# The final norm's sums in token form between the last scatters, and a PSUM bank of their own for the router's sums

## The chip, the cores and the metric

The kernel runs on one core of one Trainium2 chip. Time is device microseconds (us) of one execution. Three timed runs of the kernel before gave 1637.0, 1640.71 and 1640.89 us; the median is 1640.71. A separate execution was profiled.

## The reference, cut to what matters

256 tokens of width 1024 pass through a first network (two layers of feed-forward, mixer, feed-forward) and a second block that ends in a mixture of experts and a final norm. Only the end of the second block is touched:

```
h2  = modulate(rmsnorm(x, g_ffn), sh2, sc2)
out = x + gt2 * hier_moe(h2)          # 32 experts in 4 groups, 2 experts per token
y   = modulate(rmsnorm(out, g_final), shf, scf)
rmsnorm(x, g) = x * rsqrt(mean(x*x, over the 1024 features) + 1e-6) * g
```

Both norms need, for each of the 256 tokens, the mean of 1024 squares, then the power -1/2 of it.

## The kernel before, in words

Activations lie with features on partitions: `self.x[0..7]` are eight tiles of 128 features x 256 tokens. A sum over features is therefore a sum over partitions, which TensorE does. There are two forms of it. In token form (`sums_tok`, line 432) a half of a square tile (128 features x 128 tokens) is the stationary operand and `mean1`, one column of 1/1024, the moving one; the result has tokens on partitions and one column for each half, so 2 columns. `rsqrt_tok` (438) adds epsilon on VectorE (tile `rtt`) and takes the power on GpSimd (tile `rte`), `bcast` (445) brings the two columns back to all partitions with two matmuls against the identity. In broadcast form, as `final` (2020) does it, `mean1` broadcast to 128 x 128 is stationary and the whole square tile moves; the result is the mean on every partition, 256 columns wide, and the power is taken on that form.

An fp32 matmul stands in the trace as two or more pieces. All matmul helpers go through one line, 233, so lines say little and tiles say more.

The router. `out_proj` calls `post2` (1608) for each of the 8 feature tiles. It adds to x, scales to `u`, squares into a running sum, and leaves a closure `later` that computes the router's logits (into the bank `pr`, tag p1, 36 columns a token half) and the transposes of `u`; a tile's closure is called in the next tile's `post2`, the last one by `block2` (1100). Before, the token sums of the norm went into columns 128 and 129 of the same bank `pr`, ahead of the last closure in the program. `moe` (1638) starts with `rsqrt_tok` on these two columns, scales the logits by it on VectorE, and picks groups and experts in a chain of small VectorE steps that ends in the mask `msk`. While VectorE does that, TensorE has `WARM[0]` matmuls without use (`keep_warm`, 1631). Then TensorE counts the mask into `pk` (tag p1 as well; each tag has two banks in turn), `WARM[1]` more follow, and the gather matmuls (`oh`, `hhi`, `hlo`) collect each expert's tokens.

The experts. `moe_round` (1899) runs 11 passes of 2 or 4 experts. Weights come in 1 MB loads on SP's queue, each into a buffer of a ring that a matmul frees. A pass has the up product, `mid`, the down product, which ends in `yh` (ScalarE) and `yl` (VectorE), and the scatter, which adds the result into four PSUM banks. The last pass is cut in quarters: `down` of quarter q is followed by the scatter of quarter q-1, two feature tiles each, and VectorE adds them to x. Before, `final` then squares x on ScalarE and sums it in broadcast form, behind the last `down` in TensorE's queue, takes the power, multiplies x by it, and applies gain and shift on ScalarE and GpSimd; five stores write the output. A loop after that runs another round when an expert has more tokens than its capacity.

Order on each engine is set by a scheduler that follows the program and the operands' readiness; `issue_after(ins)` puts what stands in it behind `ins` in that engine's queue.

Of the kernel before, what the change touches and what calls it, by code (L numbers as in the profile page):

```python
# [21 lines left out]
F32 = mybir.dt.float32  # L22
# [3 lines left out]
AF = mybir.ActivationFunctionType  # L26
OP = mybir.AluOpType
# [3 lines left out]
P = 128  # L31
S = 256
D = 1024
KD = 8
NFF = 22
EPS = 1e-6
# [5 lines left out]
BIG = 2.0 ** 20  # L42
OUT_POOL, OUT_ENDS = (1, 3, 5), (0, 2, 4, 6, 7)
X_LOADS = (0, 1), (2, 3, 4), (5, 6, 7), ()
WARM = 26, 5, 6
NEARLY = 2
NAHEAD = 10
NMORE = 3
# [133 lines left out]
class Net:  # L182
# [917 lines left out]
    def block2(self, post):  # L1100
        nc, A = self.nc, self.A
        rest = self.block2_in()
        with self.tc.tile_pool(name="b2", bufs=1, reuse_waits="tile") as bp:
            T = lambda n, shape, dt=F32: bp.tile(list(shape), dt, name="b2_" + n)
            y = [bp.tile([P, S], F32, tag="y", bufs=8, name=f"b2_y{c}") for c in range(8)]
            yb, yr = y[0:4], y[4:8]
            th = [self.xp.tile([P, S], F32, tag=f"x{c}", name=f"th{c}") for c in range(8)]
            th += [T(f"th{c}", (P, S)) for c in range(8, 16)]

            def sink(c, p):  # L1110
                self.act(th[c - 20], p[:, :S], AF.Tanh, scale=0.5)

            low = lambda: bp.tile([P, S], F32R, tag="y", bufs=8, name=self.name("b2_l"))

            def second(yl):

                for d in range(KD):
                    if d % 4 == 0:
                        w = self.split_w(A["pab"][2 + d // 4], 2048)
                    p = self.bank("p1")  # L1120
                    for k in range(4):
                        self.mm3(p[:, :S], *w((d % 4 * 4 + k) * P), *yl[k], k == 0, k == 3)
                    self.stt(th[2 * d + 1], th[2 * d + 1], 1.0, p[:, :S], op0=OP.add, op1=OP.mult)
                    if d % 2:
                        yield

            with self.tc.tile_pool(name="b2m", bufs=1, reuse_waits="tile") as mp:
                self.mixers2(mp, yr, yb, sink, rest, low, second)
            self.moe_pre()
            self.expert_ring(NAHEAD, "we")  # L1130
            with self.tc.tile_pool(name="b2o", bufs=1, reuse_waits="tile") as op:
                ya = [self.split_to((op.tile([P, S], F32R, name=f"b2_ha{c}"), low()), yr[c]) for c in range(4)]
                ms = [self.xhl(d) for d in range(KD)]
                for d in range(KD):
                    if d % 4 == 0:
                        w = self.split_w(A["pab"][d // 4], 2048)
                        self.expert_ahead(PABA)
                    p = self.bank(f"p{2 + d % 2}")
                    for k in range(4):
                        self.mm3(p[:, :S], *w((d % 4 * 4 + k) * P), *ya[k], k == 0, k == 3)  # L1140
                    t = self.tmp("t3")
                    self.stt(t, th[2 * d], 1.0, p[:, :S], op0=OP.add, op1=OP.mult)
                    tg = t, th[2 * d + 1]
                    m = self.tmp("sq", bufs=4)
                    self.tt(m, tg[0], tg[1], OP.add, eng=nc.gpsimd)
                    h, l = ms[d]
                    self.act(h, m, AF.Copy, scale=0.5)
                    self.stt(l, m, 0.5, h.bitcast(F32), op0=OP.mult, op1=OP.subtract)
                    if d == 5:
                        for k in range(KD):  # L1150
                            self.x[k] = self.xp.tile([P, S], F32, tag=f"x{k}", name=f"xr{k}")
                            nc.sync.dma_start(self.x[k], self.xd[:, k])
            self.out_proj(A["w_out2"], ms, lambda d, p: post(d, p, bp.tile([P, S], F32, tag="y", bufs=8, name=f"b2_u{d}")))
            self.summed = self.sums_tok(self.acc["n"], self.pr[:, 128:130], False)
            self.later()
            self.spare = self.bank("p2"), ms[0][0]

    def mixers2(self, mp, yr, yb, gate, rest, low, second):
# [472 lines left out]
    def keep_warm(self, n):  # L1631
# [4 lines left out]
        return last  # L1636

    def moe(self, final):
        nc, A = self.nc, self.A
        pr = self.pr  # L1640
        rt = self.rsqrt_tok(pr[:, 128:130], EPS, 2)
        self.rings += [(self.st, "s")] * 3 + [(self.xp, "xl")]
        self.expert_ahead()
        self.wkb_es.close()
# [2 lines left out]
        with self.tc.tile_pool(name="moe", bufs=1, reuse_waits="tile") as mp:  # L1647
# [4 lines left out]
            n = [0]  # L1652
# [56 lines left out]
            with self.tc.issue_after(self.summed.ins):  # L1709
                self.keep_warm(WARM[0])  # L1710
            pk = self.bank("p1")
# [6 lines left out]
            with self.tc.issue_after(counted.ins):  # L1718
                self.keep_warm(WARM[1])
            self.rc = T("rc", (P, 4, 32))  # L1720
# [58 lines left out]
                return order  # L1779

            self.moe_round(weights)
            self.spare = self.bank("p1"), self.yh
            with self.tc.issue_after(self.scattered.ins):
                self.keep_warm(WARM[2])
            final()
            n_more = nc.values_load(nxi[0:1, 0:1], min_val=0, max_val=3)
            with self.tc.For_i(0, n_more, 1):
# [111 lines left out]
    def moe_round(self, early=None):  # L1899
# [69 lines left out]
        def down(n, c0=0, c1=D, w=None):  # L1969

            (heT, _, cs), (p, m, cap) = mids[n], PASSES[n]
            w = w or self.expert_get(*[(1, p + i, 0) for i in range(m)])
            for c in range(c0, c1, 512):
                e = min(c + 512, c1)
                py = self.bank("p0")
                for f in range(2):
                    for i in range(m):
                        last = self.mm(py[i * cap:(i + 1) * cap, 0:e - c], heT[:, f * P + i * cap:f * P + (i + 1) * cap],
                                       w[i].rearrange("p (q f c) -> p f q c", f=2, c=256)[:, f, c // 256:e // 256], f == 0, f == 1)
                self.act(self.yh[:, c:e], py[:, 0:e - c], AF.Copy, scale=cs)  # L1980
                self.stt(self.yl[:, c:e], py[:, 0:e - c], cs, self.yh.bitcast(F32)[:, c:e], op0=OP.mult, op1=OP.subtract)
            return w, last

        def scatter(n, ds=range(KD)):
            ohT = mids[n][1]
            for d in ds:
                o = acc[d // 2][:, (d % 2) * S:(d % 2 + 1) * S]
                first, last = n == 0 and d % 2 == 0, n == N - 1
                self.mm(o, self.yh[:, d * P:(d + 1) * P], ohT, first, False)
                self.scattered = self.mm(o, self.yl[:, d * P:(d + 1) * P], ohT, False, last)  # L1990
# [16 lines left out]
            if n < N - 1:  # L2007
                down(n)
        w = None
        for q in range(5):  # L2010
            if q < 4:
                w, last = down(N - 1, q * 256, (q + 1) * 256, w)
            if q:
                with self.tc.issue_after(last.ins):
                    scatter(N - 1, (2 * q - 2, 2 * q - 1))
                for d in (2 * q - 2, 2 * q - 1):
                    self.stt(self.x[d], acc[q - 1][:, (d % 2) * S:(d % 2 + 1) * S], self.M(5)[:, d:d + 1], self.x[d])
        self.downed = last

    def final(self, out):  # L2020
        p = self.bank("p1")
        sq = []
        for k in range(KD):
            sq.append(self.xp.tile([P, S], F32, tag=f"xh{k}", name=self.name("sq")))
            self.act(sq[-1], self.x[k], AF.Square)
        with self.tc.issue_after(self.downed.ins):
            for k in range(KD):
                self.mm(p[:, :S], self.mean1.to_broadcast([P, P]), sq[k], k == 0, k == KD - 1)
        ms, r = self.tmp("t0"), self.tmp("t1")
        self.ts(ms, p[:, :S], EPS, op0=OP.add)  # L2030
        self.tt(r, ms, self.mhalf.to_broadcast([P, S]), OP.pow, eng=self.nc.gpsimd)
        o = self.st.tile([P, KD, S], F32, tag="s", name=self.name("o"))
        for k in range(KD):
            ok = o[:, k]
            self.tt(ok, self.x[k], r, OP.mult)
            g, b = self.gF[:, k:k + 1], self.M(6)[:, k:k + 1]
            if k in OUT_POOL:
                self.ts(ok, ok, g, b, op0=OP.mult, op1=OP.add, eng=self.nc.gpsimd)
            else:
                self.act(ok, ok, AF.Identity, bias=b, scale=g)  # L2040
            if k in OUT_ENDS:
                a = max([-1] + [e for e in OUT_ENDS if e < k]) + 1
                self.nc.sync.dma_start(out[:, a:k + 1], o[:, a:k + 1])
# [180 lines left out]
```

## Time and profile before

| | before |
|---|---|
| median of the timed runs | 1640.71 us |
| the profiled execution, and its span | 1642.62 us, 1640.9 us |
| TensorE busy | 1530.8 us, 93% |
| VectorE busy | 1049.1 us, 64% |
| ScalarE busy | 696.9 us, 42% |
| GpSimd busy | 362.3 us, 22% |
| mean granted TensorE clock | 0.973 |
| DMA | 344.33 MB, mean 210 GB/s |

Times are in microseconds from the start of the span. PE is TensorE, PEld its weight load, DVE VectorE, ACT ScalarE, POOL GpSimd, SP the engine that issues most DMAs (SPq its queue). A busy TensorE isn't TensorE at its peak, since matmuls are pipelined. The granted clock (PEclk) is 1.00 at the upper of two levels and 0.50 at the lower one.

### The profile page before, as it was taken

What the parts mean: (1) busy time and instruction counts of PE and PEld (TensorE: products, weight loads), DVE (VectorE), ACT (ScalarE), POOL (GpSimd) and SP (SyncE); (2) the same over time, 40 slices, a digit from 0 to 9 for tenths busy, and PEclk for the clock granted to TensorE, in tenths of its full rate; (3) what the DMA queues carried; (4) which work ended last, traced back from release to release, by engine and by line L of the source; (5) the groups of instructions that cost most, each with busy time, mean ns of one, the idle gap of its engine ahead of it and who ended that gap; (6) DMA issues with size and microseconds to landing.
All of it is one profiled execution on the core that took longest, in us unless ns stands there. A gap on an engine that the chain in (4) does not pass through costs nothing.

```text
span 1640.9 us, 29888 instructions
## 1 busy us (share of the span) xinstructions
PE 1530.8 (93%) x11892; PEld 1359.1 (83%) x11892; DVE 1049.1 (64%) x1938; ACT 696.9 (42%) x1241; POOL 362.3 (22%) x338
## 2 busy tenths in 40 slices
PE   8999998999999999999999999998999989999760
PEld 8999996799999999999879999988888886444330
DVE  6777776867876577766987777657875474322120
ACT  5444444544444444444554456444474332111010
POOL 4131222132221112111122221233221130000027
PEclk9999999999999999999999999999999999999985
DMA  8675554145755567545334774463421298999940
GB/s 302 247 270 202 200 197 155 52 136 212 277 216 175 200 232 275 204 169 182 120 109 165 268 274 170 142 246 107 156 65 52 78 373 319 376 420 420 420 185 27
DMA packets 62482, 344.33 MB, mean 210 GB/s; under 512 B 11136, under 2 KB 15360, under 8 KB 28544
## 3 DMA queue, kind: packets, MB, share of 16 engines
q1 hardware_dynamic: 59520, 340.65, 56.2%
q8 instruction: 95, 1.56, 0.4%
q0 software_dynamic: 640, 1.57, 0.4%
q10 hardware_dynamic: 2176, 0.13, 0.1%
q14 instruction: 51, 0.42, 0.1%
HBM read 339.05 MB, written 2.36 MB: 208 GB/s over the span
## 4 chain that ended last, share of the span: by engine, by line
PE 69%; issue 15%; DVE 8%; POOL 4%; ACT 2%; DMA 1%; SPq 0%; ACTq 0%; DVEq 0%; POOLq 0%
PE ps L233 68%; POOL t L239 3%; DVE l L239 2%; PE ps L236 1%; ACT h L258 1%; DVE xl L248 1%; DVE t L239 0%; POOL rte L239 0%; DVE xh L243 0%; DMA s<-in_ev_win 0%; DVE t L248 0%; POOL sq L239 0%; POOL kne L239 0%; DVE x L239 0%; DMA x<-in_xT 0%
## 5 line engine op out<-in xcount | busy, mean ns | idle before, releaser
L233 PE MATMUL ps<-xh,h 128*128 128x256 f32 x1992 | 570.2, 286 | 12.1 <-ACT h L258 7.3
L233 PE MATMUL ps<-xh,l 128*128 128x256 f32 x1992 | 570.0, 286 | 0.2 <-DVE l L239 0.2
L233 PE MATMUL ps<-xl,h 128*128 128x256 f32 x1992 | 569.0, 286 | 0.4
L258 ACT ACTIVATE h<-s 128x1024 fp32r<-128x1024 f32 (+4 forms) x419 | 401.5, 960 | 366.0 <-PE ps L233 291.1
L239 DVE TENSOR_TENSOR l<-s,h 128x1024 fp32r<-128x1024 f32 (+4 forms) x416 | 464.7, 1125 | 139.5 <-ACT h L258 137.8
L233 PEld LDWEIGHTS ps<-xh,h 128*128 128x128 f32 x1992 | 380.5, 191 | 17.1 <-ACT h L258 6.8
L233 PEld LDWEIGHTS ps<-xh,l 128*128 128x128 f32 x1992 | 380.4, 191 | 6.1 <-DVE l L239 2.1
L233 PEld LDWEIGHTS ps<-xl,h 128*128 128x128 f32 x1992 | 380.8, 191 | 1.7 <-DVE xl L248 1.2
L239 POOL TENSOR_TENSOR t<-t,t 128x256 f32<-128x256 f32 x93 | 121.2, 1304 | 399.0 <-DVE t L239 338.3
L233 PE MATMUL ps<-ah,h 128*128 128x256 f32 x704 | 201.4, 286 | 0.0
L233 PE MATMUL ps<-ah,l 128*128 128x256 f32 x704 | 199.3, 283 | 0.1
L233 PE MATMUL ps<-al,h 128*128 128x256 f32 x704 | 199.1, 283 | 0.0
L233 PEld LDWEIGHTS ps<-ah,l 128*128 128x128 f32 x704 | 134.9, 192 | 0.4 <-DVE l L239 0.3
L233 PEld LDWEIGHTS ps<-al,h 128*128 128x128 f32 x704 | 135.0, 192 | 0.0
L233 PEld LDWEIGHTS ps<-ah,h 128*128 128x128 f32 x704 | 134.9, 192 | 0.0
L233 PE MATMUL ps<-we,gT 128*32 128x512 f32 (+1 forms) x512 | 98.8, 597 | 7.6 <-DMA we<-in_w 7.6
L239 DVE TENSOR_TENSOR t<-ps,rb 128x256 f32<-128x256 f32 x196 | 81.8, 420 | 32.3 <-PE ps L233 24.7
L239 POOL TENSOR_TENSOR t<-t,mhalf 128x256 f32<-128x256 f32 x1 | 41.1, 41127 | 223.2 <-DVE t L243 223.2
L258 ACT ACTIVATE ah<-t 128x256 fp32r<-128x256 f32 x88 | 36.7, 417 | 117.2 <-POOL t L239 117.2
L239 DVE TENSOR_TENSOR al<-t,ah 128x256 fp32r<-128x256 f32 x88 | 37.9, 431 | 64.0 <-ACT ah L258 64.0
L239 POOL TENSOR_TENSOR sa<-sa,sq 128x256 f32<-128x256 f32 x34 | 41.9, 1232 | 149.8 <-ACT sq L258 149.4
L233 PEld LDWEIGHTS ps<-we,gT 128*32 128x32 f32 (+1 forms) x512 | 25.9, 119 | 58.4 <-issue 43.1
(490 smaller groups left out, 2162.2 us busy)
## 6 DMA issues: line engine op xcount, KB each, us to landing
s<-in_ffn_gu SPq DMA_DIRECT2D x87, 1024.0 KB
we<-in_w SPq DMA_DIRECT2D x64, 1024.0 KB
s<-in_ffn_dn SPq DMA_DIRECT2D x64, 704.0 KB
we<-in_w2e SPq DMA_DIRECT2D x28, 1024.0 KB
s<-in_w_ada SPq DMA_DIRECT2D x24, 1024.0 KB
s<-in_w_in SPq DMA_DIRECT2D x18, 1024.0 KB
s<-in_w_ada_f SPq DMA_DIRECT2D x8, 1024.0 KB
s<-in_ev_win SPq DMA_DIRECT2D x7, 1024.0 KB
```

What stands on the lines that cost most here:

```text
L233: return self.nc.tensor.matmul(out, lhsT, rhs, start=start, stop=stop, skip_group_check=True)
L236: self.nc.tensor.transpose(out, in_, ident)
L239: return (eng or self.nc.vector).tensor_tensor(out, a, b, op=op)
L248: self.nc.vector.scalar_tensor_tensor(out, a, s, b, op0=op0, op1=op1)
L258: self.nc.scalar.activation(out, a, f, **kw)
```

## The change

`final`'s norm goes to token form: `moe_round` squares x and sums it in three groups of feature tiles (0 to 3 behind the scatter of tiles 4 and 5, then 4 and 5 behind the last scatter, then 6 and 7), `final` takes the power of 2 columns and broadcasts it. The router's sums get a bank of tag p1, and the last `later` closure is queued behind them. The counts of warming matmuls change, and the last ones move from `moe` into `moe_round`, behind the sums.

```
-WARM = 26, 5, 6
+WARM = 40, 6, 4
 # block2
-            self.summed = self.sums_tok(self.acc["n"], self.pr[:, 128:130], False)
-            self.later()
+            self.sums = self.bank("p1")
+            self.summed = self.sums_tok(self.acc["n"], self.sums)
+            with self.tc.issue_after(self.summed.ins):
+                self.later()
 # moe
-        rt = self.rsqrt_tok(pr[:, 128:130], EPS, 2)
+        rt = self.rsqrt_tok(self.sums[:, 0:2], EPS, 2)
...
             self.moe_round(weights)
-            self.spare = self.bank("p1"), self.yh
-            with self.tc.issue_after(self.scattered.ins):
-                self.keep_warm(WARM[2])
             final()
 # moe_round
-        for q in range(5):
+        p = self.bank("p1")
+        for q in range(6):
             if q < 4:
                 w, last = down(N - 1, q * 256, (q + 1) * 256, w)
-            if q:
+            if 0 < q < 5:
                 with self.tc.issue_after(last.ins):
                     scatter(N - 1, (2 * q - 2, 2 * q - 1))
                 for d in (2 * q - 2, 2 * q - 1):
                     self.stt(self.x[d], acc[q - 1][:, (d % 2) * S:(d % 2 + 1) * S], self.M(5)[:, d:d + 1], self.x[d])
-        self.downed = last
+            for d in {3: (0, 1, 2, 3), 4: (4, 5), 5: (6, 7)}.get(q, ()):
+                sq = self.xp.tile([P, S], F32, tag=f"xh{d}", name=self.name("sq"))
+                self.act(sq, self.x[d], AF.Square)
+                with self.tc.issue_after(self.scattered.ins):
+                    for j in range(2):
+                        summed = self.mm(p[:, j:j + 1], sq[:, j * P:(j + 1) * P], self.mean1, d + j == 0, d == KD - 1)
+        self.sums = p
+        self.spare = self.bank("p1"), self.yh
+        with self.tc.issue_after(summed.ins):
+            self.keep_warm(WARM[2])
 # final
-        p = self.bank("p1")
-        for k in range(KD):
-            sq.append(self.xp.tile([P, S], F32, tag=f"xh{k}", name=self.name("sq")))
-            self.act(sq[-1], self.x[k], AF.Square)
-        with self.tc.issue_after(self.downed.ins):
-            for k in range(KD):
-                self.mm(p[:, :S], self.mean1.to_broadcast([P, P]), sq[k], k == 0, k == KD - 1)
-        self.ts(ms, p[:, :S], EPS, op0=OP.add)
-        self.tt(r, ms, self.mhalf.to_broadcast([P, S]), OP.pow, eng=self.nc.gpsimd)
+        pb = self.bcast(self.rsqrt_tok(self.sums[:, :2], EPS, 2), "p0")
...
-            self.tt(ok, self.x[k], r, OP.mult)
+            self.tt(ok, self.x[k], pb[:, :S], OP.mult)
```

## Rows read from the trace of the kernel before

**Rows 1.** Windows: busy us (count) per engine, granted clock, DMA share, GB/s.

```profile
1400.00:1408.00 8.00, 8.00 (x38) 2.62 (x35) 1.59 (x3) 1.47 (x3) 0.00 (x0) 1.00 0.55 209
1408.00:1572.00 164.00, 152.20 (x932) 68.89 (x930) 37.94 (x97) 22.23 (x42) 0.00 (x0) 1.00 1.01 419
1587.70:1628.80 41.10, 0.00 (x0) 0.00 (x0) 0.00 (x1) 0.00 (x0) 41.06 (x1) 0.54 0.00 1
```

**Rows 2.** Waits of SP's queue, 1362 to 1412: total us, times, longest.

```profile
SPq L1874 <- PE ps L233: 27.8, 7, 11.9
```

**Rows 3.** Timeline of GpSimd and VectorE: start, us, instruction, [idle before <- releaser].

```profile
1307.46 1.01 POOL L239 TENSOR_TENSOR gne<-gnt,mhalf 128x4 f32<-128x4 f32 x1 [32.12 <-DVE gnt L243]
...
1587.64 41.13 POOL L239 TENSOR_TENSOR t<-t,mhalf 128x256 f32<-128x256 f32 x1 [223.22 <-DVE t L243]
1628.80 2.97 DVE L239 TENSOR_TENSOR o<-xr,t 128x256 f32<-128x256 f32 x8 [41.24 <-POOL t L239]
```

**Rows 4.** Timeline of the last scatters, squares and sums, three engines.

```profile
1580.94 0.28 PE L233 MATMUL ps<-t,yl 128*128 128x256 f32 x1
1581.79 0.38 PE L233 MATMUL ps<-t,yh 128*128 128x256 f32 x1 [0.57 <-ACT yh L258]
...
1582.53 0.28 PE L233 MATMUL ps<-t,yh 128*128 128x256 f32 x1
1582.65 0.28 PE L233 MATMUL ps<-t,yl 128*128 128x256 f32 x1
...
1583.48 3.61 PE L233 MATMUL ps<-sq,mean 128*128 128x256 f32 x16
...
1582.17 1.68 DVE L248 SCALAR_TENSOR_TENSOR xr<-ps,mod,xr 128x256 f32<-128x256 f32 x4
1587.13 0.43 DVE L243 TENSOR_SCALAR t<-ps 128x256 f32<-128x256 f32 x1 [3.29 <-PE ps L233]
...
1582.68 1.61 ACT L258 ACTIVATE sq<-xr 128x256 f32<-128x256 f32 x4 [0.94 <-DVE xr L248]
```

**Rows 5.** Timeline of the router's sums, warming matmuls and epsilon.

```profile
1362.45 0.50 PE L233 MATMUL ps<-mean,sq 128*128 128x1 f32 x4
...
1363.26 0.31 PE L236 MATMUL ps<-con,b_u 128*128 128x128 f32 x1
1363.32 3.35 PE L233 MATMUL ps<-xh 128*128 128x256 f32 x26
...
1363.47 0.16 DVE L243 TENSOR_SCALAR rtt<-ps 128x2 f32<-128x2 f32 x1 [1.51 <-PE ps L233]
```

**Rows 6.** Timeline of two powers and their broadcasts at block 2's start.

```profile
1074.70 0.69 POOL L239 TENSOR_TENSOR rte<-rtt,mhalf 128x2 f32<-128x2 f32 x1
...
1074.77 1.61 PE L233 MATMUL ps<-con,rte 128*128 128x128 f32 x8 [1.24 <-POOL rte L239]
...
1075.52 0.38 ACT L258 ACTIVATE rb<-ps 128x256 f32<-128x256 f32 x1 [3.14 <-PE ps L233]
```

**Rows 7.** Instructions by tile: ns shortest/median/longest, first and last start.

```profile
L239 POOL TENSOR_TENSOR rte<-rtt,mhalf x9: 685/722/1797, 18.1 to 1363.7; 128x2 f32<-128x2 f32 x9
...
L239 DVE TENSOR_TENSOR t<-ps,rb x196: 403/419/426, 22.3 to 1003.7; 128x256 f32<-128x256 f32 x196
...
L239 DVE TENSOR_TENSOR o<-xr,t x8: 410/418/617, 1628.8 to 1631.4; 128x256 f32<-128x256 f32 x8
```

**Rows 8.** Windows of the first gather, and after the last sums.

```profile
1369.40:1372.70 3.30, 3.21 (x14) 3.02 (x14) 3.24 (x13) 0.83 (x2) 0.00 (x0) 0.50 0.99 410
1587.10:1591.50 4.40, 0.00 (x0) 0.00 (x0) 0.43 (x1) 0.00 (x0) 3.86 (x1) 0.96 0.03 7
```

**Rows 9.** Timeline of TensorE: the mask's count and the first gather.

```profile
1368.41 0.19 PE L233 MATMUL ps<-moe_msk,masks 128*128 128x64 bf16 x1 [1.74 <-DVE moe_msk L239]
...
1370.39 0.58 PE L233 MATMUL ps<-oh,hlo 128*128 128x256 f32 x1
...
1372.95 0.28 PE L233 MATMUL ps<-oh,hlo 128*128 128x256 f32 x1
```

More of the change, by code (lines that the diff above doesn't have):

```diff
@@ L2017, in moe_round @@
                     self.stt(self.x[d], acc[q - 1][:, (d % 2) * S:(d % 2 + 1) * S], self.M(5)[:, d:d + 1], self.x[d])
-        self.downed = last
-    def final(self, out):
-        p = self.bank("p1")
-        sq = []
-        for k in range(KD):
-            sq.append(self.xp.tile([P, S], F32, tag=f"xh{k}", name=self.name("sq")))
-            self.act(sq[-1], self.x[k], AF.Square)
-        with self.tc.issue_after(self.downed.ins):
-            for k in range(KD):
-                self.mm(p[:, :S], self.mean1.to_broadcast([P, P]), sq[k], k == 0, k == KD - 1)
-        ms, r = self.tmp("t0"), self.tmp("t1")
-        self.ts(ms, p[:, :S], EPS, op0=OP.add)
-        self.tt(r, ms, self.mhalf.to_broadcast([P, S]), OP.pow, eng=self.nc.gpsimd)
+            for d in {3: (0, 1, 2, 3), 4: (4, 5), 5: (6, 7)}.get(q, ()):
[8 more added lines that the diff above has]
+            self.keep_warm(WARM[2])
+    def final(self, out):
+        pb = self.bcast(self.rsqrt_tok(self.sums[:, :2], EPS, 2), "p0")
         o = self.st.tile([P, KD, S], F32, tag="s", name=self.name("o"))
```

## The prediction

> **What bounds the kernel now.** I read the windows of the expert stage first [rows 1]. From 1408 to 1572 us the DMA engines are full (share 1.01, 419 GB/s): the experts' weights set the pace. Just before, from 1400 to 1408, they are at 0.55, and the load queue's waits of 1362 to 1412 [rows 2] name TensorE (27.8 us in 7 waits): a load goes out when a matmul has freed its buffer. So what the router's part of TensorE gains before 1408 is handed on to the load stream and from there to the end. The third window, 1587.7 to 1628.8, holds one instruction: TensorE 0, ScalarE 0, GpSimd 41.06 of 41.10 us. The timeline names it [rows 3]: a power of 41.13 us on GpSimd, and 0.03 us after its end VectorE's first output multiply, which had waited 41.24 us for it. From there to the end of the span, 1640.9, are 12.1 us of output stage and stores. Two stretches decide the change: the router, 1361 to 1373, and the end, from 1580.
>
> **The power.** The old one has all 256 tokens in the columns of every partition; the new one has tokens on partitions and 2 columns. Three widths stand in the trace [rows 3, 7]: 2 columns 0.72 us (the median of nine, 0.69 to 1.80), 4 columns 1.01, 256 columns 41.13. From 2 to 4 a column costs 0.15 us, from 2 to 256 it costs (41.13 - 0.72) / 254 = 0.159: the time is in the columns. The one of 4 columns came after 32.12 us of idle GpSimd, so idleness isn't it. Nothing lies beside these 41 us. Removed: 40.4 us; 39.3 if the new one is as slow as the slowest of the nine.
>
> GPSIMD Engine Reference, section "Elementwise — side-by-side cycle accounting", in the Trainium skill gives a two-input elementwise instruction about 2.6 cycles an element at 1.2 GHz. By it 256 columns would be 0.55 us (an estimate from that page), 40 us would be no matter of columns, and the edit would save half a microsecond; for this operation [rows 3, 7] contradict it, and what it would mean is rival C. Perfetto Trace Analysis, section "GPSIMD Engine Instruction", also in the Trainium skill, calls a GpSimd instruction's span unreliable; here VectorE's start right at its end [rows 3] confirms the 41 us by another engine.
>
> **The sums ahead of it.** Before, TensorE ends the last scatter at 1582.65 + 0.28 = 1582.93, does 6 warming matmuls, then 16 pieces of sums, 1583.48 to 1587.09; VectorE adds epsilon from 1587.13, and the power starts at 1587.64 [rows 4, 3]. After, a square has four pieces of one column; such a group took 0.50 us at the router [rows 5], so eight squares need 4.0 us, no less than the 3.61 of before. What is won is place: the sums of the first four squares (2.0 us) can go behind the second-last scatter, which ends at 1580.94 + 0.28 = 1581.22. TensorE then waited 0.57 us for its operand [rows 4]; that gap hides a part, the rest delays the last scatter. In numbers: these sums to 1583.22; the last scatter's four matmuls 0.12 apart, the first two done at 1583.62, all at 1583.86; VectorE's two last additions (1.68 / 4 = 0.42 each) end at 1584.5, ScalarE's two last squares (1.61 / 4 = 0.40) at 1584.95. TensorE is later than that: sums of squares 4 and 5 to 1584.86, of 6 to 1585.36, of 7 to 1585.86. Then two columns of epsilon (0.16, [rows 5]) and the power, each with 0.05 to 0.07 to start: the power runs from 1586.14 to 1586.85, 1.5 us earlier than now.
>
> Added behind the power: the broadcast back over partitions, two fp32 matmuls. At 1074 us the same step was 0.75 us from TensorE's start to ScalarE's read of its result [rows 6]; with 0.05 to start, 0.80, and the first multiply is at 1587.65 instead of 1628.80: minus 41.15. The multiplies now read PSUM; that costs nothing (0.419 us from PSUM, 0.418 from SBUF, [rows 7]), so the last 12.1 us stay. Queued behind the multiplies are the same ScalarE and GpSimd steps and the five stores as before; no DMA is added or moved.
>
> Bounds of this part. Best: the last scatter isn't delayed, squares end at 1582.68 + 1.61 = 1584.29 and only the last group stands behind them: the power 1.1 us earlier than worked out, minus 42.2. Worst: all eight groups after the last square (4.0 us from 1584.95, 3.1 later than worked out), the slowest power (1.1 more) and the broadcast at half clock (0.75 more): minus 36.2. Half clock is possible since TensorE has little to do around the power; but before, after its last matmul at 1587.1, the granted clock was still 0.96 over the next 4.4 us [rows 8], and the gap will now be about 1 us.
>
> The four warming matmuls (4 x 0.13 = 0.5 us, from 3.35 / 26 in [rows 5]) stand between the sums and the broadcast while epsilon and power run (0.99 us): hidden, 0.5 us if not. The bank for the sums, p1, and the one for the broadcast, p0, belong to expert outputs read before: no wait.
>
> **The router.** Before, the sums share a bank with the router's logits, and the epsilon step starts at 1363.47, though the last sums end at 1362.45 + 0.50 = 1362.95 [rows 5]: it waits for the last logits in the same bank. With a bank of their own, and `later` queued behind them, it can start at 1363.0: 0.47 us earlier, and with it the chain to the mask, which let TensorE's count go at 1368.41 [rows 9]. The logits and transposes moved behind the sums keep their end, about 1363.5, and are needed at 1363.9; if they came later than that, they would eat the gain. `pk` now reuses the logits' buffer instead of a fresh one; its last reader is done microseconds before.
>
> The warming matmuls go from 26 to 40. The 26 ran from 1363.32 to 1366.67; then TensorE did nothing for 1.74 us [rows 9], and from 1369.4 to 1372.7 its granted clock was 0.50, the lower of its two levels, 1.2 GHz [rows 8]. The 40 last 40 x 0.129 = 5.15 us, to 1368.5, and issue until about 1368.2. The mask is ready at 1367.9: it waits 0.3 us behind them, so TensorE gains 0.2 us there. If the clock then stays at 2.4 GHz, the gather's 13 matmuls from 1370.39 to 1372.95, 0.213 us apart [rows 9], go 0.12 apart as in the last scatter: 12 x 0.093 = 1.1 us. I take 1.2 for both together, handed on whole to the load stream [rows 1, 2]. Bounds: 0.47 + 1.1 = 1.6 gained, or 0.1 lost, if the clock falls all the same and 14 x 0.129 = 1.8 us of new matmuls fill a gap of 1.74.
>
> **Sum.** 41.15 + 1.2 = 42.4 us off the profiled execution, 1642.6 (span 1640.9): 1600.2. That execution lay 1.9 us above the median 1640.7, so 1598.3 on the median's scale; I say 1598. With both parts at their ends it would be 1596.9 to 1604.6; the shown runs go down to 1637.0, 3.7 us below the median.
>
> **Rivals.**
> A. The sums stay late: TensorE's queue has them all behind the last scatter, or the squares come late on ScalarE. For: the squares stand on ScalarE's queue among the last `yh` steps, and a queue in order can stand before an operand. Against: the edit ties the first group to the second-last scatter alone. Price 3.1 us and up to 0.75 for the clock: 1602.
> B. The router gains nothing, that is, the change does not keep the clock there: the 1.74 us gap is filled, but one-column sums and other small matmuls surround it. Price 1.2: 1599.5.
> C. The 41 us are not in the columns. The power would still take 41.13, start 1.5 us earlier, have 0.8 us behind it, and the router give 1.2: 1640.7 - 1.9 = 1638.8, no change to be seen. Against: [rows 3, 7].
> D. Slower: a second expert round. The loop after the output runs once for each capacity overflow, now never. If the router's sums, moved from a bank that the logits open to one that they open themselves, came out otherwise, a count over its capacity (64, for the smaller experts 32) would start a round: from the first gather matmuls, about 1369.5, to the last addition, 1583.85, 214 us, and a second output stage of some 14: 1598 + 228 = 1826. It decides from one token over capacity. Against: the same products are added in the same order.
>
> **How the numbers follow.** Forecast 0.62, A 0.14, B 0.20, C 0.02, D 0.02. The range goes from 1637.0 - 42.4 = 1594.6 to A and a little over it, 1602.5, and holds B. About 0.3% (4.9 us) is what a measurement of this kernel can tell from no change: faster 0.96 (forecast, A, B), same 0.02 (C), slower 0.02 (D).
>
> **What would show it.** In the profile after: a two-column GpSimd power of about 0.7 us near 1585; eight groups of one-column sums, four of them ahead of the last scatter; VectorE's first multiply about 0.8 us after the power; the output stage still 12 us. At the router: the epsilon step some 0.5 us earlier, no TensorE gap before the count, a granted clock of 1.00 through the first gather, and the full DMA stretch starting about 1.2 us earlier. The prediction is wrong if the last power keeps more than a few microseconds, if the sums all stand behind the last scatter (A), or if the load stream does not move with the router (B).

## The result, and the profile after

Four timed runs of the changed kernel gave 1599.18 to 1602.66 us, median 1601.87, beside 1639.22 (1637.0 to 1640.89) for the kernel before: ratio 0.977, 95% interval 0.9751 to 0.9789. In a second series it was 1598.53 beside 1639.67, ratio 0.9749 (0.9727 to 0.9771). The profiled execution took 1602.33 us, its span is 1600.6. The gain is 37 us in the one series and 41 in the other.

Busy time by engine on the page after (share of the span, count of instructions):

```profile
PE 1533.1 (96%) x11925; PEld 1361.7 (85%) x11925; DVE 1049.0 (66%) x1938; ACT 696.7 (44%) x1241; POOL 320.6 (20%) x338
```

Only GpSimd changed by much: 362.3 - 320.6 = 41.7 us less. The power is 40.43 of them; most of the rest is its three steps of the output stage, which take 1.80 us together instead of 2.83. VectorE's multiplies beside them now read PSUM; no run shows whether that is why. GpSimd's timeline before, then after:

```profile
1629.74 2.83 POOL L245 TENSOR_SCALAR o<-o,pre_gF,mod 128x256 f32<-128x256 f32 x3 [0.98 <-DVE o L239]
1588.09 1.80 POOL L245 TENSOR_SCALAR o<-o,pre_gF,mod 128x256 f32<-128x256 f32 x3 [2.25 <-DVE o L239]
```

The router after the change, timeline of VectorE and TensorE, against [rows 5, 9]; the first line is the router's last addition to x, from which I count:

```profile
1361.92 0.48 DVE L248 SCALAR_TENSOR_TENSOR xr<-ps,mod,xr 128x256 f32<-128x256 f32 x1 [2.59 <-PE ps L233]
...
1363.77 0.16 DVE L243 TENSOR_SCALAR rtt<-ps 128x2 f32<-128x2 f32 x1 [0.98 <-PE ps L233]
...
1364.22 5.03 PE L233 MATMUL ps<-xh 128*128 128x256 f32 x40
1369.09 0.20 PE L233 MATMUL ps<-moe_msk,masks 128*128 128x64 bf16 x1
...
1372.42 0.28 PE L233 MATMUL ps<-oh,hlo 128*128 128x256 f32 x1
```

The epsilon step (`rtt`) starts 1.85 us after the addition; the count has no idle time in brackets any more. The last `oh,hlo` of the gather comes 3.33 us after the count's start (before 1372.95 - 1368.41 = 4.54).

Windows after: the gather, the stretch before the full DMA engines, the full stretch, and two about the last power (columns as in [rows 1]):

```profile
1369.40:1372.70 3.30, 3.08 (x24) 2.72 (x25) 3.28 (x13) 0.84 (x2) 0.00 (x0) 1.00 1.01 417
1400.00:1408.00 8.00, 8.00 (x39) 2.94 (x36) 1.94 (x5) 1.76 (x3) 0.00 (x0) 1.00 0.63 233
1408.00:1572.00 164.00, 152.68 (x932) 68.79 (x931) 37.75 (x96) 22.17 (x42) 0.00 (x0) 0.99 1.01 419
1584.90:1585.90 1.00, 0.70 (x5) 0.40 (x4) 0.15 (x1) 0.00 (x0) 0.70 (x1) 0.61 0.00 0
1585.90:1587.10 1.20, 1.20 (x4) 0.91 (x4) 0.00 (x0) 0.00 (x0) 0.00 (x0) 0.50 0.00 0
```

The clock over the gather is 1.00 instead of 0.50 [rows 8]; the expert stage still runs at the DMA engines' full share. The last two windows, 0.61 and 0.50, were not foreseen. The load stream follows the router, as predicted: SP's issue of the two loads just ahead of the full stretch starts 43.33 us behind the router's last addition before and 41.95 after, 1.38 earlier (SP's timeline before, then after):

```profile
1404.41 2.93 SPq L1874 DMA_DIRECT2D we<-in_w2e  x2
1403.87 2.93 SPq L1873 DMA_DIRECT2D we<-in_w2e  x2
```

The end after, timelines of TensorE, VectorE and GpSimd, against [rows 3, 4]:

```profile
1580.24 0.28 PE L233 MATMUL ps<-t,yl 128*128 128x256 f32 x1
1580.36 1.84 PE L233 MATMUL ps<-mean,sq 128*128 128x1 f32 x16
1582.06 0.36 PE L233 MATMUL ps<-t,yh 128*128 128x256 f32 x1
...
1582.62 0.95 PE L233 MATMUL ps<-mean,sq 128*128 128x1 f32 x8
1583.80 1.05 PE L233 MATMUL ps<-mean,sq 128*128 128x1 f32 x8 [0.24 <-ACT sq L258]
1584.72 0.86 PE L233 MATMUL ps<-yh 128*128 128x256 f32 x4
1585.89 1.22 PE L233 MATMUL ps<-con,rte 128*128 128x128 f32 x4 [0.30 <-POOL rte L239]
...
1584.89 0.16 DVE L243 TENSOR_SCALAR rtt<-ps 128x2 f32<-128x2 f32 x1 [1.20 <-PE ps L233]
1587.15 2.74 DVE L239 TENSOR_TENSOR o<-xr,ps 128x256 f32<-128x256 f32 x8 [2.09 <-PE ps L233]
...
1585.13 0.70 POOL L239 TENSOR_TENSOR rte<-rtt,mhalf 128x2 f32<-128x2 f32 x1 [220.41 <-DVE rtt L243]
```

The first line is the last matmul of the second-last scatter; four groups of sums (16 pieces) stand right behind it, then the last scatter, then the other four. The power takes 0.70 us instead of 41.13.

The same points, read from the timelines of every run, cut the span into stages whose sum is the span. X is the start of the router's last addition to x (1361.08 before), S the start of the last matmul of the second-last scatter (1580.94 in [rows 4]):

| run | X | epsilon, X+ | first up product, X+ | S, X+ | last scatter, S+ | power, S+ | power | to first multiply | multiply to end | span |
|---|---|---|---|---|---|---|---|---|---|---|
| before | 1361.08 | 2.39 | 12.09 | 219.86 | 0.85 | 6.70 | 41.13 | 0.03 | 12.10 | 1640.9 |
| changed | 1361.92 | 1.85 | 10.70 | 218.32 | 1.82 | 4.89 | 0.70 | 1.32 | 13.45 | 1600.6 |
| changed, second series | 1361.19 | 1.86 | 10.73 | 218.39 | 1.82 | 4.90 | 0.70 | 1.31 | 13.41 | 1599.9 |
| end alone | 1359.89 | 2.39 | 12.01 | 219.67 | 1.82 | 5.71 | 0.70 | 1.31 | 11.82 | 1599.1 |
| router alone | 1360.53 | 1.85 | 10.70 | 218.26 | 0.85 | 6.70 | 41.13 | 0.03 | 12.25 | 1638.9 |
| 66 columns | 1357.71 | 1.85 | 10.71 | 218.26 | 1.82 | 4.90 | 10.91 | 1.31 | 14.01 | 1607.1 |
| sums late | 1359.94 | 1.85 | 10.71 | 218.27 | 0.85 | 7.25 | 0.69 | 1.32 | 12.33 | 1599.8 |
| 26 warming | 1358.68 | 1.86 | 10.53 | 218.20 | 1.82 | 4.90 | 0.70 | 1.31 | 11.81 | 1595.6 |
| shared bank, 40 warming | 1358.49 | 2.39 | 11.05 | 218.77 | 1.82 | 5.71 | 0.69 | 1.32 | 12.42 | 1597.4 |
| 9 warming behind the sums | 1359.59 | 1.85 | 10.71 | 218.28 | 1.82 | 4.90 | 0.69 | 1.32 | 11.22 | 1596.0 |
| 128-column sums | 1362.33 | 1.85 | 10.71 | 218.08 | 1.82 | 5.00 | 0.70 | 0.80 | 12.49 | 1599.4 |
| combined | 1360.96 | 1.85 | 10.52 | 218.27 | 0.84 | 4.54 | 0.71 | 0.80 | 12.72 | 1598.0 |

By stages the change is 218.32 - 219.86 = -1.54, 4.89 - 6.70 = -1.81, 0.70 - 41.13 = -40.43 and 1.32 - 0.03 = +1.29: -42.5 us up to the first multiply. The two spans differ by only 40.3, since the unchanged code ahead of X was 0.84 later and the output stage 1.35 longer. Both move between runs whose code there is the same: X from 1357.7 to 1362.3, the output stage from 11.2 to 14.0. So parts of a few us are read from the stages, and totals only carry the power.

### The profile page after: what moved, and what is told of

It reads as the page before. It is cut to its first block, busy times and chain, and to the rows that moved or that the text cites. A ratio compares the mean times of both kernels' runs of the same rounds, so it can differ in the third digit from the quotient of the medians.

```text
span 1600.6 us, 29956 instructions
## 1 busy us (share of the span) xinstructions
PE 1533.1 (96%) x11925; PEld 1361.7 (85%) x11925; DVE 1049.0 (66%) x1938; ACT 696.7 (44%) x1241; POOL 320.6 (20%) x338
## 4 chain that ended last, share of the span: by engine, by line
PE 71%; issue 15%; DVE 8%; POOL 2%; ACT 2%; DMA 1%; ACTq 0%; SPq 0%; DVEq 0%; POOLq 0%
PE ps L233 70%; DVE l L239 2%; PE ps L236 1%; ACT h L258 1%; DVE xl L248 1%; POOL rte L239 1%; DVE t L239 1%; POOL t L239 0%; DVE xh L243 0%; DMA s<-in_ffn_gu 0%; DMA s<-in_ev_win 0%; DVE t L248 0%; POOL sq L239 0%; POOL kne L239 0%; DVE x L239 0%
## 5 line engine op out<-in xcount | busy, mean ns | idle before, releaser
L248 DVE SCALAR_TENSOR_TENSOR ada<-s,ca,ada 128x1024 f32<-128x1024 f32 x56 | 71.5, 1278 | 0.0
```

Of the source, the lines that this page charges most:

```text
L248: self.nc.vector.scalar_tensor_tensor(out, a, s, b, op0=op0, op1=op1)
```

## Experiments

**The two halves.** The new end with the old router, and the new router with the old end (5 and 12 timed runs):

```
 # end alone: the changed kernel with
-WARM = 40, 6, 4
+WARM = 26, 5, 4
-            self.sums = self.bank("p1")
...
+            self.summed = self.sums_tok(self.acc["n"], self.pr[:, 128:130], False)
+            self.later()
...
 # router alone: the kernel before with
-WARM = 26, 5, 6
+WARM = 40, 6, 6
+            self.sums = self.bank("p1")
...
```

> The final norm's part of the change alone; the router's bank and its warming counts as before (26, 5). Theory: the end gives all but 1.4 us of the change, so about 1601.9 + 1.4 = 1603.3 on the scale of the changed kernel's median, some 36 us below the kernel before. In the trace: the power of 2 columns 0.7 us; at the router the epsilon step 2.4 us after the start of the last addition to x (2.39 before, 1.85 with the whole change), a TensorE gap of about 1.7 us ahead of the count, and a granted clock of 0.50 in the first gather. Rival: the router's part gives nothing that lasts; then this run is no slower than the changed kernel, within 0.3 us by the trace from the last addition of the router to the last scatter.

> The router's part alone (own bank for the sums, `later` behind them, warming 40 and 6); the final norm as before, with 256 columns. Theory: 1.2 to 1.5 us below the kernel before, too little for a total to tell from no change (0.3%, 4.9 us), but to be read in the trace: from the start of the router's last addition to x to the first up matmul 10.7 us instead of 12.1, and the same 1.4 us at the load that followed TensorE at 1408 us. The power stays at 41.1 us. Rival: the shift is lost in the load stream, and the last scatter stands 221.6 us behind the router's last addition, as before, instead of 220.2.

The end alone: 1600.89 us beside 1640.5, ratio 0.9765 (0.9748 to 0.9782). The router alone: 1640.18, ratio 0.9992 (0.998 to 1.0004), which a total can't tell from nothing; its stages show S 1.60 us earlier and everything behind unchanged. The gain is the end's, as worked out, and the router's stands in the stages but is smaller than the scatter of the totals. One thing was unforeseen in the end alone: the last group of sums took 1.87 us, in the changed kernel 1.05.

```profile
1583.12 1.87 PE L233 MATMUL ps<-mean,sq 128*128 128x1 f32 x8 [0.24 <-ACT sq L258]
```

**A power of 66 columns.** Is the price in the columns (rival C)? 64 columns of ones are put behind the two:

```
-        pb = self.bcast(self.rsqrt_tok(self.sums[:, :2], EPS, 2), "p0")
+        ms, r = self.tmp("t0"), self.tmp("t1")
+        self.nc.vector.memset(ms[:, 2:66], 1.0)
+        self.ts(ms[:, 0:2], self.sums[:, 0:2], EPS, op0=OP.add)
+        self.tt(r[:, 0:66], ms[:, 0:66], self.mhalf.to_broadcast([P, 66]), OP.pow, eng=self.nc.gpsimd)
+        pb = self.bcast(r, "p0")
```

> The changed kernel with the final power over 66 columns: 2 of sums and 64 of the constant 1, whose results nothing reads. Theory (the time is in the columns, 0.159 us each): the power takes 0.72 + 64 x 0.159 = 10.9 us and the kernel is 10.2 us slower than the changed one, about 1612. Rival (the 41 us belonged to something else, the width is nearly free): the power stays under 1.5 us and the time at 1602.

Measured 1607.7 us (ratio 0.9802, 0.9783 to 0.9822), and in the timeline of GpSimd:

```profile
1580.87 10.91 POOL L239 TENSOR_TENSOR t<-t,mhalf 128x66 f32<-128x66 f32 x1 [220.36 <-DVE t L243]
```

0.72 + 64 x 0.159 = 10.90 was to be had if every column costs what the three widths in [rows 3, 7] say. Rival C falls. The total came out some 4 us under the 1612 expected. The stages carry the price: the power takes 10.91 - 0.70 = 10.21 us more than in the changed kernel, and from X to the end of the span the profiled execution takes 249.4 instead of 238.7 us; its X lay 4.2 us earlier, in code that is the same. The Trainium skill (GPSIMD Engine Reference, "Elementwise — side-by-side cycle accounting") has about 2.6 cycles an element for a two-input instruction, which is some 0.14 us for 66 columns, an estimate from that page; this power's 10.91 us is not of that kind.

**Sums late.** All 32 pieces behind the last scatter (rival A made true):

```
+        sqs = []
...
+                sqs.append(sq)
+        with self.tc.issue_after(self.scattered.ins):
+            for d, sq in enumerate(sqs):
...
```

> The changed kernel with all eight groups of one-column sums behind the last scatter. Theory: the last scatter starts about 0.9 us earlier (in the changed kernel it started at 1582.06, 1.5 us after the end of the second-last one; its operand was there 0.5 us after that end), but TensorE then has 16 one-column pieces more behind it, 0.115 us each; the last sum ends 0.9 us later than in the changed kernel, so 1602.8, which a total can't tell. In the trace: from the end of the second-last scatter to the power's start 5.5 us instead of 4.6. Rival: the place of the sums doesn't matter because ScalarE's squares end last; then the power starts 0.5 us earlier.

The last scatter starts at S + 0.85 as before, the power at S + 7.25 instead of 4.89: 2.4 us, where the expectation had 0.9 and the prediction's price was 3.1. The total, 1603.12 (ratio 0.9761, 0.9736 to 0.9787), doesn't show it. TensorE's timeline tells why it cost that much:

```profile
1580.03 5.15 PE L233 MATMUL ps<-mean,sq 128*128 128x1 f32 x32
```

32 pieces at the pace of the changed kernel's first sixteen (1.84 / 16 = 0.115) are 3.7 us; here 5.15, and these 1.45 us on top of the expected 0.9 make the 2.4. The windows over them show the clock go down while TensorE is busy all the time:

```profile
1580.54:1582.54 2.00, 2.00 (x17) 2.00 (x17) 0.57 (x2) 1.02 (x3) 0.00 (x0) 0.83 0.00 0
1582.54:1583.94 1.40, 1.40 (x8) 1.40 (x8) 0.00 (x0) 0.00 (x0) 0.00 (x0) 0.50 0.00 0
```

**Why the broadcast took 1.2 us.** In the changed kernel it ran at a clock of 0.50. The clock had fallen before the gap around the power: 0.61 over 1584.90 to 1585.90 means, with two levels, 0.78 us at the lower one, so from about 1585.12, when the four warming matmuls (1584.72 + 0.86 = 1585.58) were still running. Two ways to keep the clock: more warming matmuls behind the sums, or sums that are 128 equal columns wide, for which `mean1` is broadcast as the moving operand.

```
 # 9 warming behind the sums
-WARM = 40, 6, 4
+WARM = 40, 6, 9
 # 128-column sums
-                        summed = self.mm(p[:, j:j + 1], sq[:, j * P:(j + 1) * P], self.mean1, d + j == 0, d == KD - 1)
+                        summed = self.mm(p[:, j * P:(j + 1) * P], sq[:, j * P:(j + 1) * P], self.mean1.to_broadcast([P, P]), d + j == 0, d == KD - 1)
...
```

> The changed kernel with 9 warming matmuls behind the last sums instead of 4. Theory (the clock falls because of the one-column sums ahead, not for want of matmuls behind them): the clock is 0.50 at the broadcast as with 4, the 9 take about 2 us at that clock and end behind the power, so that the first output multiply comes 1.8 to 2.5 us after the power (1.32 with 4). Rival (the cut from 6 to 4 let the clock fall): the clock is 1.00 at the broadcast and the multiply comes 0.8 to 1.0 us after the power.

> The changed kernel with the same sums in 128 equal columns instead of one (the moving operand is the column of 1/1024 read 128 times; columns 0 and 128 of the result are used). Theory: a piece costs the same 0.115 us, since its weight load sets the pace, but TensorE's array works through it, and the clock stays at 1.00 until the broadcast: power 4.9 us after the second-last scatter's last matmul, first multiply 0.8 us after the power instead of 1.32. In all 0.5 us, in the trace alone (1601.4). Rival: wide pieces cost more (0.22 us each, as the 256-column pieces of the kernel before), and the power comes 2 us later.

Nine warming matmuls (one profiled run, 1597.74 us), TensorE's timeline and two windows:

```profile
1582.35 1.51 PE L233 MATMUL ps<-yh 128*128 128x256 f32 x9
1583.66 1.08 PE L233 MATMUL ps<-con,rte 128*128 128x128 f32 x4
...
1582.87:1583.87 1.00, 1.00 (x8) 1.00 (x7) 0.00 (x0) 0.00 (x0) 0.59 (x1) 0.72 0.00 0
1583.87:1584.87 1.00, 0.87 (x4) 0.57 (x3) 0.09 (x1) 0.00 (x0) 0.00 (x0) 0.50 0.00 0
```

The clock fell in the midst of them, with TensorE busy for the whole first window and no idle time ahead of the broadcast, which ran at 0.50 and took 1.08 us. So the theory's clock held, and its delay did not: the nine took 1.51 us instead of about 2, and the multiply still started 1.32 after the power, not 1.8 to 2.5. The wide sums (1598.7, ratio 0.9744, 0.9728 to 0.976):

```profile
1580.52 1.95 PE L233 MATMUL ps<-mean,sq 128*128 128x128 f32 x16
...
1582.79 2.35 PE L233 MATMUL ps<-mean,sq 128*128 128x128 f32 x16
1584.89 0.72 PE L233 MATMUL ps<-yh 128*128 128x256 f32 x4
1586.16 0.71 PE L233 MATMUL ps<-con,rte 128*128 128x128 f32 x4 [0.56 <-POOL rte L239]
```

Its windows from the epsilon step to the broadcast's end:

```profile
1584.90:1586.10 1.20, 0.70 (x7) 0.50 (x5) 0.16 (x1) 0.00 (x0) 0.69 (x1) 1.00 0.00 0
1586.10:1587.00 0.90, 0.71 (x4) 0.52 (x4) 0.09 (x1) 0.00 (x0) 0.01 (x1) 1.00 0.00 0
```

Sixteen pieces take 1.95 us instead of 1.84, so 128 columns cost hardly more than one; the granted clock stays 1.00 until behind the broadcast, which takes 0.71, and the multiply follows the power by 0.80, the predicted number. The idle time ahead of the broadcast is here even longer, 0.56 us against 0.30. So it was not the gap around the power that brought the clock down, but the one-column sums ahead of it, in which TensorE is busy by its record. The price is on the same table: with 128 columns the power comes 0.11 later (S + 5.00), so that 0.41 of the 0.52 us is left.

**Which edit keeps the clock at the router.** 26 warming matmuls with the sums' own bank, and 40 with the shared bank, one profiled run each:

```
 # 26 warming
-WARM = 40, 6, 4
+WARM = 26, 6, 4
 # shared bank, 40 warming
-            self.sums = self.bank("p1")
...
+            self.summed = self.sums_tok(self.acc["n"], self.pr[:, 128:130], False)
+            self.later()
...
```

> The changed kernel with 26 warming matmuls at the router instead of 40; the sums keep their own bank. Theory (the 26 leave TensorE idle for 1.2 us before the count, and the clock falls after that as it did before): the count starts 6.8 us after the router's last addition to x (7.17 with 40), the granted clock of the first gather is 0.50 at least in part, and the first up matmul stands at 11.5 us (10.70 with 40, 12.09 in the kernel before). Rival: the gain of 1.4 us is the earlier epsilon step alone; then the clock stays at 1.00 and the up matmul comes at 10.4 us.

> The changed kernel with the router's sums back in the logits' bank (program order as before) and the 40 warming matmuls kept. It separates the two edits at the router: the earlier epsilon and the clock. Times counted from the start of the router's last addition to x. Theory (a clock that stays up is worth most of the gain, and either edit alone keeps it): epsilon at 2.39 us as before, mask count about 7.1, the 40 warming matmuls end at about 7.6 to 7.8, so no gap ahead of the count and a granted clock of 1.00 over the gather; the up product starts at 10.9 to 11.1, and the second-last scatter ends 1.1 us earlier than before instead of 1.5. Rival (the earlier epsilon is what keeps the clock): the granted clock is 0.50 over the gather in spite of 40 warming matmuls, and the up product starts at about 12.0, as before. Total: 0.4 us over the changed kernel by the theory, 1.4 by the rival, neither to be seen in one time.

The count in TensorE's timeline with 26 and the own bank, with a window of its gather:

```profile
1365.48 0.20 PE L233 MATMUL ps<-moe_msk,masks 128*128 128x64 bf16 x1 [1.15 <-DVE moe_msk L239]
...
1365.98:1369.18 3.20, 2.98 (x22) 2.49 (x20) 3.20 (x13) 0.81 (x2) 0.00 (x0) 1.00 1.02 425
```

and with 40 and the shared bank, with the window of its gather:

```profile
1360.74 5.03 PE L233 MATMUL ps<-xh 128*128 128x256 f32 x40
1365.82 0.19 PE L233 MATMUL ps<-moe_msk,masks 128*128 128x64 bf16 x1
...
1365.79:1368.99 3.20, 2.96 (x24) 2.56 (x24) 3.20 (x7) 0.29 (x1) 0.00 (x0) 1.00 1.02 417
```

Both keep 1.00. With the shared bank the 40 leave no gap, and the up product comes at X + 11.05: 1.04 us of the router's 1.39 come from the clock alone. With the own bank the earlier epsilon makes the gap 1.15 us instead of 1.74 [rows 9], and the clock stays at 1.00 through it; the up product comes at 10.53, 0.17 earlier than with 40, since the count waits for no warming matmul (X + 6.80 instead of 7.17; total 1597.36 us). So my expectation of a fallen clock with 26 was wrong: either edit alone kept the clock, and having both gains it only once. With neither it fell. The same count in the end alone, 26 matmuls and the shared bank, and two windows behind it:

```profile
1367.23 0.19 PE L233 MATMUL ps<-moe_msk,masks 128*128 128x64 bf16 x1 [1.74 <-DVE moe_msk L239]
...
1367.89:1368.39 0.50, 0.48 (x4) 0.21 (x2) 0.50 (x2) 0.00 (x0) 0.00 (x0) 0.56 1.08 459
1369.00:1371.00 2.00, 2.00 (x10) 1.79 (x9) 2.00 (x11) 0.32 (x1) 0.00 (x0) 0.50 0.98 414
```

There the up product came at X + 12.01. Each of these kernels has one profile; the pair of 26 and own bank kept the clock once more in the combined kernel below, and the pair of 26 and shared bank lost it in the kernel before as well. Every kernel that kept it also has six warming matmuls behind the count instead of five, and no run separates that edit. The end alone speaks against it: 0.56 over its first window puts the fall at about 1367.95, and the five were still running there (in the timeline they take 0.93 us from 1367.36).

**Combined.** 26 warming matmuls, 128-column sums, and GpSimd, idle there, adds the squares of tiles 1 to 3 onto that of tile 0, so that no sums stand ahead of the last scatter:

```
-WARM = 40, 6, 4
+WARM = 26, 6, 4
...
+            for d in {2: (0, 1), 3: (2, 3), 4: (4, 5), 5: (6, 7)}.get(q, ()):
...
+                if d in (1, 2, 3):
+                    self.tt(sqs[0], sqs[0], sqs[d], OP.add, eng=nc.gpsimd)
+            for d in {4: (0, 4, 5), 5: (6, 7)}.get(q, ()):
...
```

> The changed kernel with three edits: 26 warming matmuls at the router instead of 40; sums 128 equal columns wide (mean1 broadcast as moving operand) in place of one column; GpSimd adds the squares of tiles 1, 2 and 3 onto that of tile 0, so that TensorE has five groups of sums in place of eight and none ahead of the last scatter. Theory: up product at 10.5 us after the router's last addition to x (10.70 in the changed kernel); the last scatter starts 0.85 us after the second-last one's last matmul instead of 1.82; the power 4.2 us after it instead of 4.89; the first multiply 0.80 us after the power starts' end instead of 1.32. Together some 1.4 us below the changed kernel: 1599 to 1600 us, ratio to before 0.974 to 0.976, which the totals can hardly tell from it; the trace can. Rival: GpSimd's additions come too late or hold VectorE up, or 26 warming matmuls let the clock fall in this run; then the up product is at 11.5 us or later, or the power starts 4.9 us or more after the second-last scatter, and nothing is gained.

1596.45 us (1595.6 to 1599.79), ratio 0.9732 (0.9714 to 0.975). TensorE and GpSimd at its end:

```profile
1580.93 0.28 PE L233 MATMUL ps<-t,yl 128*128 128x256 f32 x1
1581.05 2.45 PE L233 MATMUL ps<-mean,sq 128*128 128x128 f32 x20
1583.25 0.72 PE L233 MATMUL ps<-yh 128*128 128x256 f32 x4
...
1579.41 1.53 POOL L239 TENSOR_TENSOR sq<-sq,sq 128x256 f32<-128x256 f32 x2 [1.06 <-ACT sq L258]
1583.77 0.71 POOL L239 TENSOR_TENSOR rte<-rtt,mhalf 128x2 f32<-128x2 f32 x1 [2.83 <-DVE rtt L243]
```

Against the changed kernel the up product is 0.18 us earlier, the power 0.35 (S + 4.54, hoped for 4.2) and the multiply 0.52 closer behind it. S itself, X + 218.27, moved by 0.05 only; among the kernels with the router's own bank it scatters from 218.08 to 218.39, more than this gain. That is 0.05 + 0.35 + 0.52 = 0.9 us, of the 1.4 expected. The interval overlaps that of the changed kernel's second series and ends where that of the first begins (0.975 and 0.9751), so only the trace shows the gain. It missed 4.2 because the 20 pieces behind the last scatter run in one row from 1581.05 to 1583.50, with the epsilon step and the power (1583.77) right after them.

## Why the prediction was right, and where its steps were off

The mechanism was right, and by stages, up to the first multiply, so was the sum: -42.5 us measured, -42.4 predicted. That it fits to 0.1 us is luck: three errors of 0.3 to 0.5 us cancel, as shown below, and the output stage, which was to stay at 12.1 us, came out 1.35 longer, so that from X to the end of the span 41.1 are left. Steps that held: the power's price in its columns (-40.43 against -40.4); rival C excluded; four groups of sums ahead of the last scatter, so not rival A; the clock kept at the router, so not B; a count within capacity, so not D.

Two steps were mis-sized. **The clock around the power.** The prediction took the broadcast at 0.80 us behind the power, because TensorE would idle only 1 us there and the clock in [rows 8] was still 0.96 long after the last matmul. Measured 1.32. The half-clock price stood in the range (0.75 more, against 0.52 measured), but its reason was wrong: the rows showed a clock after 256-column sums, and the new sums have one column. **The sums.** The prediction let the first four groups begin when the second-last scatter's last matmul had ended (S + 0.28) and gave them 2.0 us, by [rows 5]. They began 0.12 behind that matmul's start, and the last scatter 1.70 behind theirs. So it began 0.46 earlier than worked out (S + 1.82, against 1583.22 - 1580.94 = 2.28), 0.16 from the overlap and 0.30 from the pace, and the power 0.3 earlier (-1.81 against -1.5). With the router's 0.3 below they cancel: +0.5 - 0.3 - 0.3.

**The router.** -1.54 at S against -1.2. The epsilon step came 0.54 earlier (0.47 predicted), the up product 1.39, and S 1.54, which agree within the 0.3 us by which S scatters: the load stream handed the gain on. The term for the clock, 1.1, measured 1.04 by itself. The step "if the 40 fill the gap the clock stays" held, but this kernel did not need the 40: with the earlier epsilon, 26 did as well, and the 40 then cost 0.17.

**The total** came out 3.9 us above the centre, at 1601.9 where 1598.0 was said, and 1598.5 in the second series. The profiled pair puts 1.35 of it into the output stage, which no part of the code explains. There SP's issue of the stores differs; by tile, shortest, median and longest ns of the five, the changed kernel and the second profile of the same:

```profile
L2042 SPq DMA_DIRECT2D out<-o x5: 348/402/1922, 1588.2 to 1592.0; - x5
```

```profile
L2042 SPq DMA_DIRECT2D out<-o x5: 348/413/1982, 1587.6 to 1591.6; - x5
```

One of five issues took 1.9 us; before, the longest was 0.40, and with nine warming matmuls behind the sums, where nothing of the output stage is changed, 0.46, with an output stage of 11.2 us. In the combined kernel it was 1.12. Over the ten profiles with the new end the three with an issue of 1.9 us or more have the three longest output stages (13.41 to 14.01; the others 11.2 to 12.7). The rival expected for the second profile, an output stage 1.3 us longer in this kernel every time, fits both its profiles (13.45 and 13.41), but with 26 warming matmuls, where only the router's count of them differs, it is 11.81. Whether the earlier end brings the slow issue about or chance is not settled, and neither is the rest of the difference between the totals (39 us as the mean of both series) and the stages' 42.5: X varies by 4.6 us in code that no kernel here changes. Also open is why the clock fell some 1.5 us earlier in the end alone and with the shared bank (power at S + 5.71 in both) than in the others with the changed kernel's end (4.9): the two have the router's shared bank in common, but by S that stage is 218 us past, and each has one profile.

## What to carry to other kernels

Put the argument of a costly per-column function (here GpSimd's power, 0.159 us a column) on partitions, and pay two small matmuls to bring it back; look for such an instruction in a window where one engine alone is busy. A matmul with one moving column isn't cheaper than one with 128 (0.115 and 0.12 us a piece here), but it can cost the clock of what follows. When two edits each would remove the same stall, try each alone: the second one may only cost.

## What was not expected of the hardware

- TensorE's granted clock went from 1.00 to 0.50 during or right behind a stream of one-column sums in which its record shows it busy (32 pieces: 5.15 us instead of 3.7; the last 8 pieces: 1.87 instead of 1.05). With 128 columns at nearly the same pace it stayed at 1.00.
- Idle time by itself did not decide: 1.15 us of gap ahead of the router's count kept 1.00 (two kernels), 1.74 us ended at 0.50 (two kernels), and 0.56 us after wide sums kept 1.00 while 0.30 us after narrow ones stood at 0.61 and 0.50.
- A store's issue on SP can take 1.9 us (three profiles of two kernels), in a stage whose median issue takes 0.34 to 0.42.
